# A hybrid decoder layer on one core: where the plain loads, the accumulating DMAs and the last merged quarter's epilogue stand

## The chip, the cores and the metric

The kernel runs on one core of a Trainium2 chip. The metric is the device time of one execution, in microseconds; the time before is 816.44 us, the median of three runs (816.44 to 817.08). The core has five engines with their own in-order streams of instructions: TensorE (PE in the profile), VectorE (DVE), ScalarE (ACT), GpSimd (POOL) and SyncE (SP). SP, ACT and POOL also issue DMAs here, and a DMA stands in its issuer's stream like any other instruction.

## What is computed

One layer on a sequence of 256 tokens of width 2048, all in float32:

```python
h = rmsnorm(x, norm_mix_g)
u = h @ w_in                                  # 12,288 columns
c_g, b_g, xa, za, q, fl, iv, og, ga, gb = split(u)   # ga, gb: 2048 each
ya = b_g * causal_dwconv3(c_g * xa, conv_w) * silu(za)
o  = hgrn2_chunked(silu(q), (1 - lb) * sigmoid(-fl), iv, log_f)
yb = rmsnorm_heads(o) * hg_norm_g * silu(og)
m  = sigmoid(ga) * (ya @ w_a_out) + sigmoid(gb) * (yb @ w_b_out)
x  = x + m @ w_o
x  = x + sigmoid(rmsnorm(x, ple_norm_g) @ w_ple_gate) * (p @ w_ple_proj)
out = rmsnorm(x, final_norm_g)
```

The time goes into the matrix products: 256 rows against some 150 MB of weights.

## The kernel before

**Products.** Each float32 operand is held as a high part and a low part, and a product of two is three matmuls: high by high, high by low, low by high (`triple`, L1038 to L1040). A matmul has 128 tokens as its stationary side and 512 weight columns as its moving side. A chunk is 256 rows of the contraction by 512 columns, for both halves of the tokens: 2 x 2 products, 12 matmuls. The program walks a list of chunks, `items`, in the order of the parts of `w_in`, then `w_a` and `w_b`, then `w_o` (kind "O", four quarters of columns of eight chunks each), then the last gate.

**Weights.** `load` sends 1 MB for two chunks (512 KB in the first stage) from SP's queue into one of three buffers `raw`. `split` calls `cut`: ScalarE writes the high part (`whi`, L169), VectorE the low part (`wlo`, L170). This runs three chunks (`LEAD`) ahead of the products, further ahead at the end. TensorE has only products to do and goes from one chunk to the next without a pause, as long as the parts are there.

**Units of seven products.** For three of the four quarters of `ga` and `gb` (j = 1, 2, 3), five of the eight chunks (c = 0, 2, 3, 5, 6) are "units", kind "S": the 2 x 2 blocks of tokens and contraction, and the `ga` and `gb` columns beside each other, are computed by seven products for eight, after Strassen and Winograd. For it sums of weights are needed, and sums of token blocks. The three other chunks (c = 1, 4, 7) are plain (kind "C"). There are 15 units.

- Sums of weights, `combine_weights`, called two items ahead of the unit. `A` (`sA`, two buffers) and `B` (`sB`, two buffers) are loaded on SP's queue. `X` (`sT`, three buffers) is formed by `add_by_dma` on POOL's queue: a plain load of 512 KB (L157) and then a DMA of 512 KB that adds to it on arrival (L163), which waits for the load to have landed. VectorE makes two sums (L701), and then `X`, `B` and `A` are each cut into parts: `thi`, `tlo` of `X`, `bhi`, `blo` of `B`, `thi`, `tlo` of `A`. There is one pair of `bhi`, `blo`. At its end `combine_weights` calls `add_by_dma()` for the next unit that has none; the first are called for at `begun + 3`, `+ 5` and `+ 7`, where `begun` is the last chunk before the units.
- Sums of tokens, `token_sums`: once, before the units, four sums for each of the five chunks, in high and low parts, `shi` and `slo`, from the parts `xh`, `xl` of the tokens (`hT`).
- `unit_products` issues the seven products of a unit in the order of `names_of`: two with `whi`, `wlo`, then the one that multiplies `bhi`, `blo` (the block B22 of the weights) with the fourth token sum, then four more.

**The merge.** When the products of `w_b` for quarter j are complete, `ep_bb` (L778) multiplies them by the gate (`gb`, L782), adds the other branch (L786), and has the result `m`. It must be turned so that its columns lie on partitions before it can multiply `w_o`. The turn goes through DRAM: four writes (`to_dram`, L304), one read back (L315), and a transposition in squares on VectorE (L308). Quarters 0 to 2 are parked in DRAM and come back later (`unpark`). The last, j = 3, goes through `turned` at once; then `put_m` makes `mh` (ScalarE, L775) and `ml` (VectorE, L776), which are the stationary sides of the products with `w_o`. The chunks of "O" use the quarters in order, so that the last quarter comes with contraction blocks 12 to 15.

**Order.** Each epilogue is a generator; `advance` lets every live one go a step, once for each chunk. What stands between two `yield`s stands together in the streams of the engines. Each engine runs its stream in order. The planner of the language then orders the instructions of each engine by its own estimate, except where dependencies are put in by hand: between `begun` and eight chunks after the last quarter of the branch products began (`parked`), `pinned` fixes the order of ScalarE and VectorE to the order in which the program was written. SP's stream in the order of the built program is, near the last quarter: a load of `w_o`, the four writes of the turn, a load of `w_o`, the readback, three loads of `w_o`.

Of the kernel before, what the change touches and what calls it, by code (L numbers as in the profile page):

```python
# [9 lines left out]
F32 = mybir.dt.float32  # L10
F32R = mybir.dt.float32r
AF = mybir.ActivationFunctionType
ALU = mybir.AluOpType
PSUM = bass.MemoryType.PSUM

P = 128
# [7 lines left out]
CW = 512  # L24
# [7 lines left out]
SEVEN = [()] + 3 * [(0, 2, 3, 5, 6)]  # L32
# [15 lines left out]
def hybrid_kernel(ctx, tc, xT, x, pT, prm, gfin, masks, w_in, w_a, w_b, w_o, w_pg, w_pp, out):  # L48
    nc = tc.nc
# [9 lines left out]
    pools, closers = {}, {}  # L59
# [13 lines left out]
    state = {"tmp": "tmp1"}  # L73
# [3 lines left out]
    def nm(s):  # L77
        uid[0] += 1
        return f"{s}_{uid[0]}"

    def t4(tag="t4", bufs=None):
        bufs = bufs or {"tmp1": 8, "tmp2": 1, "tmp3": 5}[state["tmp"]]
        return pools[state["tmp"]].tile([P, 1024], F32, tag=tag, bufs=bufs, name=nm(tag))
# [12 lines left out]
    pair_sums = {}  # L96
# [9 lines left out]
    items = []  # L106
# [16 lines left out]
    def raw_of(pos):  # L123
        it = items[pos]
        if it["raw"] not in loaded:
            if it["kind"] == "S":
                t = tuple(
                    pools["st"].tile([P, n, CW], F32, tag=tag, bufs=2, name=nm(tag)) for tag, n in (("sA", 2), ("sB", 1))
                )
            else:  # L130
                t = wp.tile([P, 2, 2 * CW], F32, tag="raw", bufs=3, name=nm("raw"))
            loaded[it["raw"]] = t
        return loaded[it["raw"]]
# [18 lines left out]
    def add_by_dma(behind=None):  # L152
        pos = next((n for n, it in enumerate(items) if it["kind"] == "S" and n not in pair_sums), None)
        if pos is not None:
            w, g, c = items[pos]["w"]
            X = pair_sums[pos] = pools["st"].tile([P, 2, CW], F32, tag="sT", bufs=3, name=nm("sT"))
            d = nc.gpsimd.dma_start(out=X.rearrange("p n x -> p (n x)"), in_=w[g + 1, :, c, :])  # L157
            if behind is not None:
                tc.add_manual_dep(
                    d.ins, behind.name,  # L160
                    mybir.DependencyInfo(mybir.DependencyClass.Sync, mybir.DependencyReason.DATA), reason="order",
                )
            nc.gpsimd.dma_start(out=X, in_=w[g : g + 2, :, c, :CW].rearrange("n p x -> p n x"), accum_op=ALU.add)  # L163

    def pair_of(pool, n, tags=("whi", "wlo"), width=2 * CW):
        return tuple(pool.tile([P, width], F32R, tag=tag, bufs=n, name=nm(tag)) for tag in tags)
# [18 lines left out]
    def combine_weights(pos):  # L185
        st = pools["st"]
        (A, B), X = raw_of(pos), pair_sums[pos]
        add(A[:, 0], X[:, 0], B[:, 0])
        add(A[:, 1], A[:, 0], A[:, 1])
        ts = []  # L190
        for n, src in enumerate((X, B, A)):
            hi, lo = pair_of(st, 1, ("bhi", "blo"), CW) if n == 1 else pair_of(st, 3, ("thi", "tlo"))
# [9 lines left out]
    begun = next(n for n, it in enumerate(items) if it["kind"] == "ga" and it["last"])  # L202
# [7 lines left out]
    prm_t = const.tile([P, PRM_N], F32, name="prm_t")  # L210
    praw = pools["tmp1"].tile([P, 1024], F32, tag="X", bufs=4, name="praw")[:, : 2 * T]
    pop = pools["tmp1"].tile([P, 1024], F32R, tag="X", bufs=4, name="pop")
# [76 lines left out]
    def blocks(ap):  # L289

        return ap.rearrange("p (c b e) -> p c b e", b=4, e=32)
# [5 lines left out]

        return ap.rearrange("p (b c t e) -> p t c b e", b=4, c=4, t=NT)[:, t]

    def to_dram(src, tag, bufs):  # L300
        d = dram.tile([P, 4, T], F32, tag=tag, bufs=bufs, name=nm(tag))
        to = d.rearrange("(b i) a x -> a i b x", b=4)
        for a in range(4):
            nc.sync.dma_start(out=to[a], in_=src[32 * a : 32 * a + 32, :].rearrange("i (b x) -> i b x", b=4))  # L304
        return d

    def square_turn(dst, src):
# [1 line left out]
            out=dst.rearrange("p (k a e) -> p a k e", a=4, e=32), in_=src.rearrange("p (a k e) -> p a k e", a=4, e=32)  # L309
        )  # L310

    def turned(src, lag, dst=None):
        d = to_dram(src, "turn", 3)
        yield
        nc.sync.dma_start(out=src, in_=d.rearrange("p a x -> p (a x)"))  # L315
        for _ in range(lag):
            yield
        dst = t4() if dst is None else dst
        square_turn(dst, src)
        return dst  # L320
# [413 lines left out]

    def token_sums():
        nu = len(SEVEN[1])
        state["S"] = pair_of(pools["st"], 1, ("shi", "slo"), nu * 4 * P)
        state["S"] = tuple(v.rearrange("p (u s t) -> p u s t", u=nu, s=4) for v in state["S"])
        yield
        yield  # L740
        for first, n in TOGETHER:
            yield
            F, S = (
                pools["st"].tile([P, 2 * CW], F32R, tag=tag, bufs=3, name=nm(tag))[:, : n * 4 * P].bitcast(F32)
                for tag in ("thi", "tlo")
            )
            c = SEVEN[1][first]
            hi, lo = (v[:, 2 * c : 2 * (c + n), :] for v in state["hT"])
            Fv = F.rearrange("p (k t) -> p k t", t=T)
            nc.vector.tensor_tensor(out=Fv, in0=hi.bitcast(F32), in1=lo.bitcast(F32), op=ALU.add)  # L750
            yield
            Fv = F.rearrange("p (u r b t) -> p u r b t", u=n, r=2, b=2)
            Sv = S.rearrange("p (u s t) -> p u s t", u=n, s=4)
            a11, a12, a21, a22 = Fv[:, :, 0, 0], Fv[:, :, 1, 0], Fv[:, :, 0, 1], Fv[:, :, 1, 1]
            s1, s2, s3, s4 = (Sv[:, :, i] for i in range(4))
            for out, u, v, op in (
                (s1, a21, a22, ALU.subtract), (s2, s1, a11, ALU.subtract),
                (s3, a11, a21, ALU.subtract), (s4, a12, s2, ALU.add),
            ):
                nc.vector.tensor_tensor(out=out, in0=u, in1=v, op=op)  # L760
            hi, lo = (v[:, first : first + n] for v in state["S"])
            nc.scalar.activation(out=hi, in_=Sv, func=AF.Copy)
            nc.vector.tensor_tensor(out=lo, in0=Sv, in1=hi.bitcast(F32), op=ALU.subtract)
            yield

    def ep_a(j, psum):
# [11 lines left out]
    def ep_bb(j, psum):  # L778
        ga, gb = state["ga"], state["gb"]
        for t in range(NT):  # L780
            s = slice(t * CW, (t + 1) * CW)
            nc.vector.tensor_tensor(out=gb[:, s], in0=gb[:, s], in1=psum[t], op=ALU.mult)  # L782
        m = t4()
        for t in range(NT):
            s = slice(t * CW, (t + 1) * CW)
            nc.vector.tensor_tensor(out=spread(m, t), in0=blocks(ga[:, s]), in1=blocks(gb[:, s]), op=ALU.add)  # L786
        if j == 3:
            m = yield from turned(m, 3, back())
            put_m(j, m)
        else:  # L790
            state["m", j] = to_dram(m, f"m{j}", 1)
            yield

    def back():
        return pools["back"].tile([P, 1024], F32, tag="back", bufs=5, name=nm("back"))
# [259 lines left out]
    def names_of(it):  # L1055
        if it["kind"] == "C":
            return [("c", it["n"], t) for i in range(2) for t in range(NT)]
        return ["P1", ("c", 0, 0), ("c", 1, 0), "P5", "P7", "P6", ("c", 0, 1)]

    def into(name, op, part):  # L1060
        left[name] -= 1
# [3 lines left out]
    def unit_products(pos):  # L1065
        it = items[pos]
        c, h = it["c"], state["hT"]

        def x_of(r, t):
            return tuple(v[:, 2 * c + r, t * P : (t + 1) * P] for v in h)  # L1070

        hi, lo = parts.pop(pos)
        halves = [(hi[:, i * CW : (i + 1) * CW], lo[:, i * CW : (i + 1) * CW]) for i in range(2)]
        names = names_of(it)
        if it["kind"] == "C":
            for n, name in enumerate(names):
                into(name, x_of(n // 2, n % 2), halves[n // 2])
            return
        b22, t1, t3, t2, t4_ = sums.pop(pos)
        s1, s2, s3, s4 = (tuple(v[:, SEVEN[1].index(c), i] for v in state["S"]) for i in range(4))  # L1080
        for name, op, part in zip(names, (x_of(0, 0), x_of(1, 0), s4, s1, s3, s2, x_of(1, 1)),
                                  (halves[0], halves[1], b22, t1, t3, t2, t4_)):
            into(name, op, part)

    def pinned(start):
# [16 lines left out]
    for pos, it in enumerate(items[:last_group]):  # L1102
        mark = len(nc.cur_bb.bb.instructions)
        kind, j, c, last = (it[n] for n in ("kind", "j", "c", "last"))
        _, _, w, g, opname = groups[it["gi"]]
# [60 lines left out]
        else:  # L1166
            if c == 0:
                psum = [bank("s" if kind == "PP" and j >= 2 else "g") for _ in range(NT)]
            hi, lo = parts.pop(pos)
            for i in range(2):  # L1170
                k = 2 * c + i
                s = slice(i * CW, (i + 1) * CW)
# [10 lines left out]
        if pos == begun:  # L1183
            finish()
            second_part()
            active.append(token_sums())
        if pos in (begun + 3, begun + 5, begun + 7):
            add_by_dma(state["splits"][0])
        if kind == "O" and j == 0 and c == nch - 3:
            finish()  # L1190
# [23 lines left out]
    for t, halves in ((0, (0, 1)), (1, (0,)), (1, (1,))):  # L1214
        bk, n = bank("g"), CW // 2
        for c in range(nlast):
# [3 lines left out]
            hi, lo = parts[last_group + c]  # L1220
            for i in range(2):
                k = 2 * c + i
                s = slice(i * CW + halves[0] * n, i * CW + (halves[-1] + 1) * n)
# [83 lines left out]
```

## Time and profile before

| | |
|---|---|
| time, median of three runs | 816.44 us (816.44 to 817.08) |
| time of the profiled execution | 816.5 us |
| its span in the trace | 814.7 us |
| TensorE busy | 803.2 us, 4059 matmuls |
| VectorE, ScalarE busy | 589.2 us, 459.4 us |
| read from HBM, written to it | 184.19 MB, 13.63 MB |
| DMA of 512 KB on POOL's queue, median from issue to landing | 8.5 us (30 issues) |
| a 1 MB load of `w_o` on SP's queue, the same | 6.1 us (16 issues) |
| a write of 128 KB for a turn, the same | 2.8 us (60 issues) |

The span begins with the first instruction of the trace and ends with the last. A row of a timeline gives the start, the duration, the engine (SPq, ACTq are the parts that issue DMAs), the line of the kernel, the operation, and what it writes and reads. In brackets stands the time that the engine sat idle just before, and what released it. The chain of waits goes back from the last instruction, at each step to what released it. A window row gives the stretch, the busy time of the engines with the number of instructions, the granted clock of TensorE, the mean share of the DMA engines that were busy, and GB/s.

### The profile page before, as it was taken

How to read it: one execution, taken by the hardware profiler on the slowest of the kernel's cores; microseconds unless marked ns; L12 is line 12 of the kernel's file. 1: busy time of each engine (PE TensorE's matmuls, PEld its weight loads, DVE VectorE, ACT ScalarE, POOL GpSimd, SP SyncE). 2: the span in 40 equal slices, each digit the busy share in tenths (PEclk: the TensorE clock that was granted, in tenths of full speed). 3: DMA queues.
4: the chain of work that ended last, by engine and by line, in shares of the span. 5: the costliest groups of instructions: out<-in, count | busy, mean ns of one | idle time of the engine just before them, and what ended most of it. 6: DMA issues, size and time to landing. Idle time of an engine off the chain costs nothing.

```text
span 814.7 us, 10651 instructions
## 1 busy us (share of the span) xinstructions
PE 803.2 (99%) x4059; PEld 665.4 (82%) x4059; DVE 589.2 (72%) x745; ACT 459.4 (56%) x614; POOL 48.5 (6%) x57
## 2 busy tenths in 40 slices
PE   9999999999999999999999999999999999999995
PEld 6888888888888888888888878888888788888885
DVE  7746588767766498767679968987988756677932
ACT  7576476466565466456455546556554546566623
POOL 1000000001000000010011110110100000001210
PEclk9999999999999999999999999999999999999998
DMA  9988555648867555648789989998944888777802
GB/s 339 392 307 288 197 201 175 233 139 267 252 237 249 198 175 196 207 157 269 259 296 282 286 268 297 284 280 260 283 163 177 291 300 300 255 274 298 276 34 103
DMA packets 52659, 198.52 MB, mean 244 GB/s; under 512 B 6784, under 2 KB 16256, under 8 KB 37888
## 3 DMA queue, kind: packets, MB, share of 16 engines
q1 hardware_dynamic: 45504, 180.54, 63.6%
q0 software_dynamic: 6240, 15.73, 8.2%
q10 hardware_dynamic: 864, 1.57, 0.5%
q8 instruction: 31, 0.51, 0.2%
q14 instruction: 20, 0.16, 0.1%
HBM read 184.19 MB, written 13.63 MB: 243 GB/s over the span
## 4 chain that ended last, share of the span: by engine, by line
PE 85%; DVE 7%; issue 4%; DMA 2%; ACT 2%; POOL 0%; POOLq 0%; DVEq 0%; ACTq 0%
PE g L1038 26%; PE g L1039 26%; PE g L1040 25%; DVE wlo L170 3%; PE s L1039 2%; PE s L1040 2%; PE s L1038 2%; DMA sT<-in_w_in 1%; DMA raw<-in_w_o 1%; PE s L484 1%; DVE sA L701 1%; ACT whi L169 0%; DVE tlo L170 0%; PE s L932 0%; DVE back L308 0%
## 5 line engine op out<-in xcount | busy, mean ns | idle before, releaser
L170 DVE TENSOR_TENSOR wlo<-raw,whi 128x1024 fp32r<-128x1024 f32 (+1 forms) x264 | 319.9, 1229 | 159.9 <-ACT whi L169 158.0
L169 ACT ACTIVATE whi<-raw 128x1024 fp32r<-128x1024 f32 (+1 forms) x264 | 272.9, 1051 | 208.1 <-PE g L1040 175.2
L1038 PE MATMUL g<-whi,xh 128*128 128x512 f32 (+1 forms) x738 | 283.8, 385 | 0.0
L1039 PE MATMUL g<-wlo,xh 128*128 128x512 f32 (+1 forms) x738 | 283.7, 384 | 0.0
L1040 PE MATMUL g<-whi,xl 128*128 128x512 f32 (+1 forms) x738 | 283.6, 384 | 0.0
L1040 PEld LDWEIGHTS g<-whi,xl 128*128 128x128 f32 x738 | 138.7, 188 | 27.8
L1038 PEld LDWEIGHTS g<-whi,xh 128*128 128x128 f32 x738 | 138.7, 188 | 27.5
L1039 PEld LDWEIGHTS g<-wlo,xh 128*128 128x128 f32 x738 | 138.7, 188 | 27.1
L1039 PE MATMUL g<-wlo,mh 128*128 128x512 f32 x128 | 49.9, 390 | 0.3 <-DVE wlo L170 0.3
L1038 PE MATMUL g<-whi,mh 128*128 128x512 f32 x128 | 49.6, 389 | 0.0
L1040 PE MATMUL g<-whi,ml 128*128 128x512 f32 x128 | 49.5, 389 | 0.0
L1040 PE MATMUL s<-whi,xl 128*128 128x512 f32 x84 | 32.7, 389 | 0.0
L1038 PE MATMUL s<-whi,xh 128*128 128x512 f32 x84 | 32.7, 389 | 0.0
L1039 PE MATMUL s<-wlo,xh 128*128 128x512 f32 x84 | 32.7, 389 | 0.0
L169 ACT ACTIVATE thi<-sA 128x1024 fp32r<-128x1024 f32 x15 | 15.9, 1063 | 25.0 <-DVE sA L701 21.3
L1039 PEld LDWEIGHTS g<-wlo,mh 128*128 128x128 f32 x128 | 24.0, 188 | 5.6 <-DVE wlo L170 0.7
L1038 PEld LDWEIGHTS g<-whi,mh 128*128 128x128 f32 x128 | 24.0, 188 | 5.1
L1040 PEld LDWEIGHTS g<-whi,ml 128*128 128x128 f32 x128 | 24.0, 188 | 5.0
L1039 PE MATMUL g<-wlo,ybTh 128*128 128x512 f32 x64 | 24.9, 389 | 0.0
L1040 PE MATMUL g<-whi,ybTl 128*128 128x512 f32 x64 | 24.9, 389 | 0.0
L1038 PE MATMUL g<-whi,yaTh 128*128 128x512 f32 x64 | 24.9, 389 | 0.0
L1039 PE MATMUL g<-wlo,yaTh 128*128 128x512 f32 x64 | 24.9, 389 | 0.0
(215 smaller groups left out, 910.2 us busy)
## 6 DMA issues: line engine op xcount, KB each, us to landing
raw<-in_w_in SPq DMA_DIRECT2D x66, 1024.0 KB, 5.0
raw<-in_w_o SPq DMA_DIRECT2D x16, 1024.0 KB, 6.1
raw<-in_w_pg SPq DMA_DIRECT2D x16, 1024.0 KB, 5.7
sT<-in_w_in POOLq DMA_DIRECT2D x30, 512.0 KB, 8.5
raw<-in_w_in SPq DMA_DIRECT2D x28, 512.0 KB, 6.9
raw<-in_w_a SPq DMA_DIRECT2D x8, 1024.0 KB, 6.4
raw<-in_w_b SPq DMA_DIRECT2D x8, 1024.0 KB, 7.7
turn<-t SPq DMA_DIRECT2D x60, 128.0 KB, 2.8
```

Of the source, the lines that this page charges most:

```text
L169: a = nc.scalar.activation(out=hi, in_=src, func=AF.Copy)
L170: v = nc.vector.tensor_tensor(out=lo, in0=src, in1=hi.bitcast(F32), op=ALU.subtract)
L484: nc.tensor.matmul(out, X[:, 0, h, s], X[:, 1, h, t], start=True, stop=True, tile_position=(0, i * n))
L701: nc.vector.tensor_tensor(out=out, in0=a, in1=b, op=ALU.add)
L1038: nc.tensor.matmul(psum, oh, hi, start=first, stop=False)
L1039: nc.tensor.matmul(psum, oh, lo, start=False, stop=False)
L1040: nc.tensor.matmul(psum, ol, hi, start=False, stop=last)
```

## The change

1. `add_by_dma` issues the plain load of a unit, and behind it the accumulation of the unit before it, which it kept in `state["adding"]`. With no more unit to load it issues the accumulation alone. There are four buffers `sT` and three `sB`, and one more call at `begun + 9`. POOL's stream becomes load 0, load 1, accumulation 0, load 2, accumulation 1, and so on. From the fifth on a load waits until `X` of the unit four before it has been cut.
2. For the room, `token_sums` keeps three of the four sums in `shi`, `slo`; the fourth goes into the places of `xh`, `xl` (the second half of the tokens, the first block of each unit's contraction) which the units' products don't read otherwise. For each of the three groups of chunks ScalarE and VectorE get one more instruction.
3. The seven products of a unit start with the one of B22 and the fourth sum; the two with `whi`, `wlo` follow.
4. In `ep_bb`, for j = 3, a `yield` stands behind the multiplication and one behind the addition, and the lag ahead of the square turn is two for three. The four writes are issued by ScalarE, the readback by POOL.

In the built program SP's stream near the last quarter is then: `w_o` loads without a break, four loads of `x` and the load of the final gain, and the next `w_o` load; the four writes stand on ScalarE ahead of the `whi` of the following pair of chunks. On VectorE one `wlo` stands between the multiplications and the additions, and the square turn stands directly ahead of `ml`. On TensorE, five matmuls of the second chunk of the next group of columns come ahead of the first that uses the last quarter, beyond those that did before.

```diff
-                    pools["st"].tile([P, n, CW], F32, tag=tag, bufs=2, name=nm(tag)) for tag, n in (("sA", 2), ("sB", 1))
+                    pools["st"].tile([P, n, CW], F32, tag=tag, bufs=bufs, name=nm(tag))
+                    for tag, n, bufs in (("sA", 2, 2), ("sB", 1, 3))
...
-            X = pair_sums[pos] = pools["st"].tile([P, 2, CW], F32, tag="sT", bufs=3, name=nm("sT"))
+            X = pair_sums[pos] = pools["st"].tile([P, 2, CW], F32, tag="sT", bufs=4, name=nm("sT"))
             d = nc.gpsimd.dma_start(out=X.rearrange("p n x -> p (n x)"), in_=w[g + 1, :, c, :])
...
-            nc.gpsimd.dma_start(out=X, in_=w[g : g + 2, :, c, :CW].rearrange("n p x -> p n x"), accum_op=ALU.add)
+        if "adding" in state:
+            w, g, c = items[state["adding"]]["w"]
+            X = pair_sums[state.pop("adding")]
+            with tc.issue_after(d.ins) if pos is not None else ExitStack():
+                nc.gpsimd.dma_start(
+                    out=X, in_=w[g : g + 2, :, c, :CW].rearrange("n p x -> p n x"), accum_op=ALU.add
+                )
+        if pos is not None:
+            state["adding"] = pos
...
-    def to_dram(src, tag, bufs):
+    def to_dram(src, tag, bufs, queue=nc.sync):
...
-            nc.sync.dma_start(out=to[a], in_=src[32 * a : 32 * a + 32, :].rearrange("i (b x) -> i b x", b=4))
+            queue.dma_start(out=to[a], in_=src[32 * a : 32 * a + 32, :].rearrange("i (b x) -> i b x", b=4))
...
-    def turned(src, lag, dst=None):
-        d = to_dram(src, "turn", 3)
+    def turned(src, lag, dst=None, queues=(nc.sync, nc.sync)):
+        d = to_dram(src, "turn", 3, queues[0])
         yield
-        nc.sync.dma_start(out=src, in_=d.rearrange("p a x -> p (a x)"))
+        queues[1].dma_start(out=src, in_=d.rearrange("p a x -> p (a x)"))
...
-        state["S"] = pair_of(pools["st"], 1, ("shi", "slo"), nu * 4 * P)
-        state["S"] = tuple(v.rearrange("p (u s t) -> p u s t", u=nu, s=4) for v in state["S"])
+        state["S"] = pair_of(pools["st"], 1, ("shi", "slo"), nu * 3 * P)
+        state["S"] = tuple(v.rearrange("p (u s t) -> p u s t", u=nu, s=3) for v in state["S"])
...
-            hi, lo = (v[:, first : first + n] for v in state["S"])
-            nc.scalar.activation(out=hi, in_=Sv, func=AF.Copy)
-            nc.vector.tensor_tensor(out=lo, in0=Sv, in1=hi.bitcast(F32), op=ALU.subtract)
+            sums_of = tuple(v[:, first : first + n] for v in state["S"])
+            fourth = tuple(v[:, 2 * c : 2 * (c + n) : 2, P:] for v in state["hT"])
+            for (hi, lo), src in ((sums_of, Sv[:, :, :3]), (fourth, Sv[:, :, 3])):
+                nc.scalar.activation(out=hi, in_=src, func=AF.Copy)
+                nc.vector.tensor_tensor(out=lo, in0=src, in1=hi.bitcast(F32), op=ALU.subtract)
...
             nc.vector.tensor_tensor(out=gb[:, s], in0=gb[:, s], in1=psum[t], op=ALU.mult)
+        if j == 3:
+            yield
...
         if j == 3:
-            m = yield from turned(m, 3, back())
+            yield
+            m = yield from turned(m, 2, back(), (nc.scalar, nc.gpsimd))
...
-        return ["P1", ("c", 0, 0), ("c", 1, 0), "P5", "P7", "P6", ("c", 0, 1)]
+        return [("c", 1, 0), "P1", ("c", 0, 0), "P5", "P7", "P6", ("c", 0, 1)]
...
-        if pos in (begun + 3, begun + 5, begun + 7):
+        if pos in (begun + 3, begun + 5, begun + 7, begun + 9):
             add_by_dma(state["splits"][0])
```

More of the change, by code (lines that the diff above doesn't have):

```diff
@@ L1079, in unit_products @@
         b22, t1, t3, t2, t4_ = sums.pop(pos)
-        s1, s2, s3, s4 = (tuple(v[:, SEVEN[1].index(c), i] for v in state["S"]) for i in range(4))
-        for name, op, part in zip(names, (x_of(0, 0), x_of(1, 0), s4, s1, s3, s2, x_of(1, 1)),
-                                  (halves[0], halves[1], b22, t1, t3, t2, t4_)):
+        s1, s2, s3 = (tuple(v[:, SEVEN[1].index(c), i] for v in state["S"]) for i in range(3))
+        s4 = x_of(0, 1)
+        for name, op, part in zip(names, (s4, x_of(0, 0), x_of(1, 0), s1, s3, s2, x_of(1, 1)),
+                                  (b22, halves[0], halves[1], t1, t3, t2, t4_)):
             into(name, op, part)
```

## The prediction, made before the changed kernel ran

> **What bounds the kernel now.** I read the page first, then TensorE's waits, then its busy time by stretches, then the timelines and the chain of waits around each gap.
>
> ```profile
> PE 803.2 (99%) x4059; PEld 665.4 (82%) x4059; DVE 589.2 (72%) x745; ACT 459.4 (56%) x614; POOL 48.5 (6%) x57
> ```
> ```profile
> 460.00:480.00 20.00, 18.95 (x84) 1.00 0.77 209
> 480.00:640.00 160.00, 160.00 (x707) 1.00 0.80 254
> 640.00:660.00 20.00, 19.71 (x87) 1.00 0.93 331
> 660.00:800.00 140.00, 140.00 (x642) 1.00 0.67 237
> 800.00:814.70 14.70, 5.99 (x50) 0.78 0.34 126
> ```
> ```profile
> PE s L932 <- DVE warm L928: 1.5, 1, 1.5
> PE s L1039 <- DVE blo L170: 1.0, 1, 1.0
> PE g L1039 <- DVE wlo L170: 0.3, 1, 0.3
> ```
>
> TensorE is busy for 803.2 of 814.7 us. Of the 11.5 us idle, 1.5 lie at the head, 8.7 in the tail (14.70 - 5.99), and 1.05 and 0.29 in two stretches; the granted clock is 1.00 in those. No matmul is removed, so only the last two are to be had. What each costs is more than its idle time, since a matmul that waits inside a product also starts its successor late:
>
> ```profile
> 474.79 0.39 PE L1038 MATMUL s<-bhi,shi 128*128 128x512 f32 x1
> 476.23 0.50 PE L1039 MATMUL s<-blo,shi 128*128 128x512 f32 x1 [1.04 <-DVE blo L170]
> 476.56 0.40 PE L1040 MATMUL s<-bhi,slo 128*128 128x512 f32 x1
> ```
> ```profile
> 646.84 0.61 PE L1038 MATMUL g<-whi,mh 128*128 128x512 f32 x2
> 647.74 0.50 PE L1039 MATMUL g<-wlo,mh 128*128 128x512 f32 x1 [0.29 <-DVE wlo L170]
> 648.08 0.40 PE L1040 MATMUL g<-whi,ml 128*128 128x512 f32 x1
> ...
> 650.15 0.40 PE L1038 MATMUL g<-whi,mh 128*128 128x512 f32 x1
> ```
>
> Columns of the timeline: start, duration, what ran, and in brackets the idle time before it. Starts of matmuls normally lie 0.226 us apart (160 us for 707, the row of 480 to 640). Stall 1: from 474.79 to 476.56 is 1.77 for two starts (0.45), so **1.32 us**. Stall 2: from 646.84 to 648.08 is 1.24 for three starts (0.68), so **0.56 us**. Together 1.88 us, 0.23% of the time. This is the most the change can gain.
>
> Where they come from, by the chain of waits, then POOL's, VectorE's and SP's timelines:
>
> ```profile
> 452.36 0.59 POOL sT L157
> ...
> 461.51 11.32 DMA sT<-in_w_in
> ```
> ```profile
> 473.02 0.69 DVE L701 TENSOR_TENSOR sA<-sT,sB 128x512 f32<-128x512 f32 x1 [4.48 <-DMA sT<-in_w_in]
> ```
> ```profile
> 639.21 6.05 DMA raw<-in_w_o
> ...
> 645.37 1.07 ACT whi L169
> ...
> 646.46 1.24 DVE wlo L170
> ```
> ```profile
> 637.33 1.78 SPq L304 DMA_DIRECT2D turn<-t  x4
> 639.21 0.39 SPq L150 DMA_DIRECT2D raw<-in_w_o  x1
> ...
> 642.84 0.34 SPq L315 DMA_DIRECT2D t<-turn  x1
> ```
>
> Stall 1: POOL issued a unit's plain load at 452.36, waited 8.6 us for it, and only then issued the accumulation, which took 11.32 us; VectorE sat 4.48 us for it. Stall 2: the 1 MB load of `w_o` stood on SP's queue behind the four writes of the last quarter, and landed 6.05 us after 639.21.
>
> **The change part by part.**
>
> *The accumulation.* A unit's accumulation now follows the plain load of the next unit, and its own load was issued one unit before. The accumulation that went at 461.51 can go right behind the issue at 452.36, at some 453.5. With its 11.32 us it lands at 464.8, and 4.48 us of idle VectorE ended at 473.02, so VectorE could first use it at 468.5: margin 3.7. What POOL is moved past is one plain load at a time; each waits for `tlo` of the unit four back, as the one before waited for that of three back. If the load beside it slows the accumulation by as much as a whole load (9.2 us, 452.36 to 461.51), it lands at 474.0, 1.2 later than before. I take the margin, which is nearest to the 11.32 seen with loads beside it: gain **1.32**, bounds a loss of 1.2 and the whole gain.
>
> *The B22 product first.* It needs `bhi`, `blo` six matmuls (1.36 us) earlier. The tile view of `blo`:
>
> ```profile
> L170 DVE TENSOR_TENSOR blo<-sB,bhi x15: 684/685/693, 441.8 to 596.7; 128x512 fp32r<-128x512 f32 x15
> L1039 PE MATMUL s<-blo,shi x15: 389/389/499, 445.1 to 600.1; 128*128 128x512 f32 x15
> ```
>
> The first pair is ready at 442.5 and used at 445.1, the last at 597.4 and used at 600.1: 2.6 and 2.7 us, so some 1.2 stays. The three more ScalarE and VectorE instructions for the fourth sum (at most 0.69 each, as `blo`) lie in the same cover. Cost 0; if a unit lacked it, at most 1.36 for that unit.
>
> *SP's queue.* With the writes gone the `w_o` load goes out when its buffer is free, behind the previous `wlo`, 1.9 us earlier (637.3 for 639.21). Then whi and wlo are 1.9 earlier against 0.9 us of stall seen: gain **0.56**, with about 1 us to spare; bounds 0 and 0.56. Four loads of `x` and the final gain now stand ahead of a later `w_o` load; with the DMA share at 0.67 from 660 on I take 0, at worst a stall of stall 2's size, 0.56.
>
> *The last quarter's epilogue.* Here is the price.
>
> ```profile
> 634.82 1.28 DVE L782 TENSOR_TENSOR gb<-gb,g 128x512 f32<-128x512 f32 x2
> 636.02 1.29 DVE L786 TENSOR_TENSOR t<-ga,gb 128x512 f32<-128x512 f32 x2
> ...
> 647.60 1.24 DVE L308 STREAM_TRANSPOSE back<-t 128x1024 f32<-128x1024 f32 x1
> ```
> ```profile
> 648.88 1.07 ACT L775 ACTIVATE mh<-back 128x1024 fp32r<-128x1024 f32 x1 [0.78 <-DVE back L308]
> 648.88 0.82 ACTq L993 DMA_DIRECT2D xs<-in_x  x2
> ```
>
> `mh` was complete at 649.95, and in program order the matmul at 650.15 is the first to use it: it was 0.2 us from being a stall itself. Now, on the same clock:
> - A `wlo` (1.24, as at 646.46, with its start overlapped 1.2) stands between the products and the sum, so the sum ends at 638.5 for 637.3.
> - Four writes on ScalarE's queue cost four issues of 0.41 (0.82 for two): issued by 640.2. The next `whi` on ScalarE waits up to 1.2 us behind them; it has three chunks of lead, 8.2 us.
> - The last write landed, before, when the readback could go, 642.84 - 639.11 = 3.7 after its issue. Nearest rows for the bounds:
>
> ```profile
> raw<-in_w_o SPq DMA_DIRECT2D x9, 1024.0 KB, 6.1
> ...
> turn<-t SPq DMA_DIRECT2D x4, 128.0 KB, 2.6
> t<-turn SPq DMA_DIRECT2D x1, 512.0 KB, 4.1
> ```
>
>   2.6 (the median write) below, 6.1 above (as long as the 1 MB load that now runs beside them). I take 3.7: 643.9.
> - The readback goes from POOL. POOL's timeline has the same 512 KB as plain loads:
>
> ```profile
> 514.11 0.59 POOL L157 DMA_DIRECT2D sT<-in_w_in  x1 [3.71 <-DVE tlo L170]
> 520.62 1.18 POOL L163 DMA_DIRECT2D sT<-in_w_in  x1 [5.91 <-DMA sT<-in_w_in]
> ...
> 565.87 0.59 POOL L157 DMA_DIRECT2D sT<-in_w_in  x1 [10.15 <-DVE tlo L170]
> 570.86 1.18 POOL L163 DMA_DIRECT2D sT<-in_w_in  x1 [4.40 <-DMA sT<-in_w_in]
> ```
>
>   6.5 and 5.0 us; I take 5.7. Below 4.1 (SP's readback), above 9.2 (the load at 452.36). Landed at 649.6.
> - Turn and `mh` take 2.35 (647.60 to 649.95): `mh` at 651.95; low 640.2 + 2.6 + 4.1 + 2.35 = 649.25, high 640.2 + 6.1 + 9.2 + 2.35 = 657.85.
>
> TensorE wants it at 650.15, less stall 2 (0.56), plus five matmuls of the next group that the new order puts ahead (1.13): 650.7. New stall: **1.2 us**, between 0 and 7.1. Behind the turn on VectorE stands only `ml` and then a `wlo` for a later chunk; behind `mh` on ScalarE two loads and a `whi`, both covered by that same lead unless the stall passes some 4 us.
>
> The Trainium skill, page "DMA: Bandwidth & Descriptors", section "Queues, rings and completion order", says that each DMA engine takes turns, a packet at a time, between the queues that have work for it. By it the writes on ScalarE's queue share the engines with the 1 MB load, where on SP's they went ahead of it; the sum by it is the slower rival's, and no row here shows two such queues at once. The same page's section on the software path gives about 2.0 us plus the bytes over 436 GB/s, an estimate of 3.2 us for the readback, by which there would be no stall and the sum would be 814.6; the 5.0 to 6.5 us above speak against it.
>
> Sum, against the profiled execution's own 816.5 us (span 814.7 and 1.8 around it; the median of the runs is 816.44, the same within 0.1): 816.5 - 1.32 - 0.56 + 1.2 = **815.8 us**.
>
> **The rivals.**
> - *Both stalls go and the quarter is in time.* It needs the chain 1.2 us shorter than my sum: writes as the median (2.6) or a readback like SP's (4.1). For it: the load that shares the engines with them now starts 1.9 us sooner, and is that much further on. Against it: before, with the better queue, 0.2 us was left. 816.5 - 1.88 = 814.6.
> - *Slower: the quarter becomes the bound.* The writes share the engines with the 1 MB load and take its 6.1, and the readback, among the loads that follow, 6.5: 640.2 + 6.1 + 6.5 + 2.35 = 655.15, a stall of 4.4: 816.5 - 1.88 + 4.4 = 819.0. It decides once the stall passes 1.88. For it, the DMA engines there are full already; the window view has
>
> ```profile
> 640.00:642.00 2.00, 2.00 (x10) 1.65 (x10) 1.85 (x2) 0.40 (x1) 0.00 (x0) 1.00 1.03 228
> ```
>
>   a DMA share of 1.03 at 228 GB/s. Against it, the transfers have been seen at 3.7 and 4.1 in this very place.
> - *The change doesn't do what it says in the first stage.* The accumulation, beside a load, lands late again, or B22 first makes a new stall of up to 1.36: stall 1 is replaced. 816.5 - 0.56 + 1.2 = 817.1. Against it the margin of 3.7 us.
>
> **How the numbers follow.** A measurement of this kernel tells about 0.2% (1.63 us) from no change. My forecast, a stall between 0.25 and 3.5, has 0.38: no change. The quarter in time has 0.33: faster. The slower rival has 0.19, and of the last (0.10) I count 0.05 as slower and 0.05 as no change. So faster 0.33, same 0.43, slower 0.24. The likeliest case's own range is 814.9 to 818.1. For 8 in 10 the range goes from just under the full gain, 814.4, to 818.8, nearly all of the slower rival's sum; the high end of the chain (7.1 us, 821.7) is left out.
>
> **What would show it.** Stall 1 right: TensorE's waits have no `blo`, and no accumulation waits for its own load for 8 us. Stall 2 right: the `w_o` load starts next to 637.3 and no wait for `wlo` follows. The quarter right: a wait of TensorE for `mh` of about 1.2 us near 651, the readback on POOL taking 5 to 6.5 us. Wrong: no wait there (faster), or one over 3.5 us (slower), or a wait for `blo` or `tlo` anywhere among the units.

## The result, and the profile after

The changed kernel takes 822.81 us, the median of six runs (821.85 to 826.62); before, beside it, 816.22 (815.64 to 817.08). The ratio is 1.0088, 95% interval 1.0066 to 1.0110: slower by 0.9%, some 6.6 us, outside the range forecast.

First the page's engine line of the changed kernel, then TensorE's waits, then its busy time by stretches (us, busy time and matmuls, granted clock, share of the DMA engines, GB/s):

```profile
PE 804.2 (98%) x4059; PEld 665.9 (81%) x4059; DVE 590.3 (72%) x748; ACT 458.7 (56%) x617; POOL 48.9 (6%) x58
```
```profile
PE g L1052 <- ACT mh L786: 7.2, 1, 7.2
PE s L946 <- DVE warm L942: 1.5, 1, 1.5
```
```profile
440.00:480.00 40.00, 40.00 (x179) 1.00 1.00 303
480.00:640.00 160.00, 160.00 (x707) 1.00 0.73 238
640.00:660.00 20.00, 12.79 (x50) 0.83 0.91 332
```

Both old waits, for `blo` and for `wlo`, are gone: 440 to 480 is full. One new wait is there, for the last quarter's `mh`, and it is 7.2 us long. The granted clock falls to 0.83 in that stretch. The timeline of TensorE shows both costs:

```profile
649.11 0.39 PE L1053 MATMUL g<-wlo,mh 128*128 128x512 f32 x1
656.71 0.79 PE L1052 MATMUL g<-whi,mh 128*128 128x512 f32 x1 [7.21 <-ACT mh L786]
657.30 0.63 PE L1053 MATMUL g<-wlo,mh 128*128 128x512 f32 x1
657.73 0.63 PE L1052 MATMUL g<-whi,mh 128*128 128x512 f32 x1
...
660.03 0.40 PE L1052 MATMUL g<-whi,mh 128*128 128x512 f32 x1
```

From 649.11 to 656.71 is 7.60 where 0.23 is due: 7.37 us lost. Then matmuls start 0.43 us apart for 0.23, and eight starts take 3.32 us for 1.81: another 1.51. The two stalls that went saved 1.88. 7.37 + 1.51 - 1.88 = 7.0, and the spans differ by 821.7 - 814.7 = 7.0: the whole loss is in this one place.

The chain of waits says what was late:

```profile
637.09 0.34 ACTq L313
...
638.43 8.73 DMA turn<-t
...
647.83 6.47 DMA t<-turn
654.32 1.26 DVE back L317
655.60 1.06 ACT mh L786
656.71 0.79 PE g L1052
```
```profile
637.09 2.68 ACTq L313 DMA_DIRECT2D turn<-t  x4
```
```profile
635.88 12.48 SPq L151 DMA_DIRECT2D raw<-in_w_o  x4
```

One of the four writes landed 8.73 us after its issue, at 647.16; counted from the end of the four issues (637.09 + 2.68 = 639.77) that is 7.4 us, where before it was 3.7. The readback on POOL took 6.47. SP meanwhile sends one 1 MB load after the other. A view of the DMA queues over 642.5 to 644 shows how the two share (queue, packets, MB, share of the 16 engines; q1 is SP's queue, q10 ScalarE's):

```profile
DMA packets 123, 0.57 MB, mean 378 GB/s; under 512 B 3, under 2 KB 61, under 8 KB 61
...
q1 hardware_dynamic: 64, 0.51, 88.1%
q10 hardware_dynamic: 59, 0.06, 11.2%
```

64 packets of SP's queue and 59 of ScalarE's: in this stretch the queues move as many packets each, as if they took turns, one for one. But a packet of the load is 8 KB and one of the writes 1 KB, so the writes get 11% of the engines' time here. It isn't so all the way. From 640 to 641 few packets of loads were moving, 20 against 298 of the writes, and the writes had 81.3% of the engines. By 642.5, 445 of their 576 packets were through; what is late is the rest, beside the loads issued at 639.4 and 643.4.

The Trainium skill, page "DMA: Bandwidth & Descriptors", section "Queues, rings and completion order", has the rule of turns between queues, packet by packet; the counts of the stretch agree. The section puts some 9 to 17 descriptors into a packet; the turns seen here are of single transfers of 8 KB and 1 KB, as the second experiment shows.

### The profile page after: what moved, and what is told of

Its sections match the earlier page's. It is cut to its first block, busy times and chain, and to the rows that moved or that the text cites. A ratio compares the mean times of both kernels' runs of the same rounds, so it can differ in the third digit from the quotient of the medians.

```text
span 821.7 us, 10659 instructions
## 1 busy us (share of the span) xinstructions
PE 804.2 (98%) x4059; PEld 665.9 (81%) x4059; DVE 590.3 (72%) x748; ACT 458.7 (56%) x617; POOL 48.9 (6%) x58
## 4 chain that ended last, share of the span: by engine, by line
PE 90%; DVE 3%; issue 2%; DMA 2%; ACT 1%; ACTq 0%; POOLq 0%; POOL 0%
PE g L1052 27%; PE g L1054 27%; PE g L1053 27%; PE s L1053 3%; PE s L1054 3%; PE s L1052 3%; DVE wlo L179 2%; DMA turn<-t 1%; DMA t<-turn 1%; DVE back L317 1%; PE s L493 1%; ACT mh L786 1%; PE s L946 0%; PE s L594 0%; ACT whi L178 0%
## 5 line engine op out<-in xcount | busy, mean ns | idle before, releaser
L1052 PEld LDWEIGHTS g<-whi,mh 128*128 128x128 f32 x128 | 24.4, 191 | 12.6 <-ACT mh L786 7.6
```

The costliest lines, as they stand in the source:

```text
L1052: nc.tensor.matmul(psum, oh, hi, start=first, stop=False)
```

## The experiments

The variants start from the changed kernel, except where the kernel before is named; times are medians, ratios go against runs of the kernel before on the same chip. Theory A: the writes are late because their queue takes turns with the loads of SP's queue. Its rivals: the readback on POOL and the extra steps (B), the later sum (C), ScalarE's queue itself (D).

**Writes back on SP's queue, the readback on POOL's.**

```diff
-            m = yield from turned(m, 2, back(), (nc.scalar, nc.gpsimd))
+            m = yield from turned(m, 2, back(), (nc.sync, nc.gpsimd))
```

> The changed kernel with the last quarter's four writes back on SP's queue (behind the w_o load that was issued first, ahead of the next one); the readback stays on POOL, the extra steps stay. Theory A (the writes are late because ScalarE's queue shares the DMA engines with two 1 MB loads on SP's queue): the last write lands about 4 us after its issue for 8.7, the readback takes 6 to 6.5 us as before, TensorE waits about 2.5 us for mh (7.2 - 4.7), time 817 to 818 us. Theory B (the readback on POOL and the extra steps are the price): the writes gain little or the chain stays long, the wait for mh is 5 us or more, time 820 or more.

817.63 us, ratio 1.0019 (1.0008 to 1.0029). Its waits, then its chain:

```profile
PE g L1053 <- DVE wlo L179: 1.8, 1, 1.8
```
```profile
639.16 3.87 DMA turn<-t
...
643.70 7.15 DMA t<-turn
...
650.87 0.04 DVE back L317
...
652.04 1.19 DVE wlo L179
```

The last write lands 3.87 us after its issue for 8.73, as A has it. The wait is not for `mh` but for a `wlo` that stands behind the square turn on VectorE: with other queues the planner also put matmuls in another order. In the built programs the first matmul with the last quarter's `mh` stands 13 places (2.9 us) later than in the changed kernel.

**The readback alone on SP's queue** (`(nc.scalar, nc.sync)`; the order of TensorE, VectorE and ScalarE up to `mh` as in the changed kernel).

> The changed kernel with the readback alone back on SP's queue; the writes stay on ScalarE's. Theory A: the writes still land some 8.7 us after the last issue; the readback at best 4.1 us and no POOL issue, so TensorE waits 4 to 7 us, time 819 to 823. Theory B: the wait for mh is under 2 us, time below 817.

820.15 us, ratio 1.0038 (1.0018 to 1.0057).

```profile
PE g L1052 <- ACT mh L786: 4.2, 1, 4.2
```
```profile
639.72 8.13 DMA turn<-t
...
647.93 3.75 DMA t<-turn
```

The writes are as late as before (8.13), the readback takes 3.75 for 6.47 and starts without POOL's 0.67 (647.16 to 647.83 in the changed kernel). So POOL's share of the wait is some 3 us and the rest the larger one; B falls as the sole cause. The ten runs go from 815.98 to 821.69, and the one profiled (821.61) is among the slowest; the three fastest, 815.98 to 817.20, leave little room for such a wait, so the write need not be this late each time.

This trace also shows the turns themselves. With the readback on SP's queue no third load follows, and from 645.8 to 647.4 the engines are nearly empty, in the view of the DMA queues (GB/s in 40 slices of 0.04 us):

```profile
GB/s 0 0 26 205 0 0 51 410 0 0 0 26 205 0 26 26 230 0 0 26 205 0 0 26 0 0 0 0 26 205 0 0 0 0 0 0 0 26 0 0
q1 hardware_dynamic: 10, 0.06, 8.6%
q10 hardware_dynamic: 14, 0.01, 2.1%
```

In a slice, 26 GB/s is one packet of 1 KB and 205 one of 8 KB. They mostly come in pairs, a small one and then a large one, less than two of the 16 engines' worth (10.7%), and the last write lands at 647.85. So the write waits for a few packets that still take turns with 8 KB ones while most engines have nothing to do; the mean share of 11% doesn't measure that. Why these are behind the others, no run here shows.

**Both on SP's queue, the extra steps kept** (`(nc.sync, nc.sync)`).

> The changed kernel with writes and readback on SP's queue, the extra steps kept. Theory A: writes about 4 us, readback 4 to 6 us, wait for mh 0 to 2 us, time 814.5 to 816.5. Theory C (the later sum, by one wlo, and the five matmuls put ahead are themselves the price): a wait of 5 us or more stays, time above 820.

814.90 us, ratio 0.9989 (0.9979 to 0.9998): faster than both kernels. No wait but the first one of the program is left to TensorE. C falls as it was put, with a wait of 5 us or more. The SP rows:

```profile
637.36 2.69 SPq L313 DMA_DIRECT2D turn<-t  x4
640.16 0.39 SPq L151 DMA_DIRECT2D raw<-in_w_o  x1
644.07 0.34 SPq L324 DMA_DIRECT2D t<-turn  x1
```

4.0 us from the end of the issues to the readback, even with one 1 MB load sent ahead of the writes. It isn't all due to that: `mh` starts only at 652.39 and ends at 653.43, which would be late by some 4 us in the changed kernel's order. Here the planner put the matmul that needs it 19 places, 4.3 us, later. From the first write's issue to the end of `mh` it is 16.1 us here, 19.6 in the changed kernel and 12.6 in the kernel before. The writes and the readback take 5.4 us less than in the changed kernel (3.4 and 2.0), but the turn, which stands behind a `wlo` on VectorE here, gives 1.9 back. So 3.5 of the 7.4 us are gone; the rest is a chain that is longer than before on SP's queue too, and only this order of TensorE hides it. To that extent C stands.

**The whole epilogue of before**, parts 1 to 3 of the change alone:

```diff
-        if j == 3:
-            yield
...
-            yield
-            m = yield from turned(m, 2, back(), (nc.scalar, nc.gpsimd))
+            m = yield from turned(m, 3, back())
```

> The changed kernel with the whole epilogue of before (no extra steps, lag 3, everything on SP): parts 1 to 3 of the change alone. All theories: stall 1 (1.32 us) is gone, stall 2 (0.56 us) stays, no wait for mh over 0.5 us: 816.2 - 1.3 = 814.9 us, 0.16% below before. If the accumulation or the B22 product first had a hidden price, it shows here as a time at or above 816.2.

815.75 us, ratio 0.9992 (0.9983 to 1.0002). The profile is as expected, a wait for `wlo` and none for `blo`; the time gained 0.2 us for 1.3 in the median, and the interval holds both.

**Longer packets, everything else in place.** The order of all instructions is that of the changed kernel.

```diff
-            queue.dma_start(out=to[a], in_=src[32 * a : 32 * a + 32, :].rearrange("i (b x) -> i b x", b=4))
+            s = slice(32 * a, 32 * a + 32)
+            queue.dma_start(out=d[s].rearrange("p a x -> p (a x)"), in_=src[s, :])
```

(for ScalarE's queue alone)

> The changed kernel, with the four writes of the last quarter laid out in DRAM row by row, so that each of the 128 rows goes as one run of 4 KB for four of 1 KB; bytes, queue and order of all instructions stay (the turn then reads a wrong layout, so the last quarter of m is not the layer's). Theory A (two queues take turns packet for packet, and a 1 KB packet waits for an 8 KB one each time): the last write lands 4 to 5.5 us after its issue for 8.7, the wait for mh is 3.5 to 5 us, time 818 to 820. Theory D (it is the bytes that share, or ScalarE's queue that is slow): the write lands after 8 us or more, time 822 to 823.

821.65 us, ratio 1.0077 (1.0054 to 1.0101). The tile's landing times (the slowest of the four writes and the readback), then TensorE's waits:

```profile
DMA to landing us min/median/max: 4.9/5.1/6.3
```
```profile
PE g L1056 <- ACT mh L790: 3.6, 1, 3.6
PE s L950 <- DVE warm L946: 1.5, 1, 1.5
PE s L1057 <- DVE blo L179: 0.6, 1, 0.6
```

With a quarter of the packets and the same bytes the slowest write takes 6.3 us for 8.7, and the wait for `mh` is half. 2.4 us of that are the write's; another 1.2 come from the readback, 5.3 for 6.47. That is A's direction, short of its 5.5, and D's "8 us or more" is out. The time is not what A forecast: the slow clock after the wait was left out of the expectation, and this profiled execution has a `blo` wait besides.

**One load held** until the writes have landed (the second of those beside them; the third stands behind it in SP's queue):

```diff
-                nc.sync.dma_start(out=raw, in_=w[g, :, c : c + 2, :])
+                d = nc.sync.dma_start(out=raw, in_=w[g, :, c : c + 2, :])
+                for before in state.pop("hold", ()):
+                    tc.add_manual_dep(
...
```

> The changed kernel, with one wait more: the second 1 MB load of w_o that ran beside the writes is held until the four writes have landed; writes on ScalarE's queue, readback on POOL's. Theory A: without that load the last write lands 3 to 4.5 us after its issue, the readback, beside the held load, takes 6 to 7.5, and TensorE waits 2.5 to 4.5 us for mh or for a weight behind it: 817 to 819. Theory D (ScalarE's queue is slow by itself): the write lands after 7 us or more, and the time is 822 or more.

821.90 us, ratio 1.0076 (1.0056 to 1.0095).

```profile
639.02 5.01 DMA turn<-t
...
644.69 8.15 DMA t<-turn
```

The write takes 5.01 for 8.73, but the held load and those behind it now run beside the readback, which takes 8.15 for 6.47. What was given up at one place is paid at the next: the wait is 5.2 us. A's forecast had the direction, but its sizes (4.5 for the write, 7.5 for the readback, 819 for the time, at most) are all passed. From 642.3 to 643.6 the last 34 packets run alone, at 7.0% of the 16 engines, about one engine's worth: here too a few packets are behind the others.

**Both loads held**, a probe of the writes alone: the first load goes behind the writes in the program, too.

> The changed kernel, with both 1 MB loads of w_o that ran beside the four writes held until the writes have landed; a probe, its time is no matter (the weights come late). Theory A: alone on the DMA engines the last write lands 2 to 3 us after the end of the issues (7.4 in the changed kernel). If ScalarE's queue is slow by itself: 4 us or more.

```profile
638.18 2.80 ACTq L319 DMA_DIRECT2D turn<-t  x4
642.96 1.96 SPq L152 DMA_DIRECT2D raw<-in_w_o  x3
```

The loads, which waited for the writes, go at 642.96, 2.0 us after the end of the issues (640.98). ScalarE's queue isn't slow: 2.0 us with no load, 4.5 with one (639.48 to 644.03), 7.3 with two (640.52 to 647.85, the readback alone on SP's queue), 7.4 in the changed kernel, where three ran beside the writes in turn (issued at 635.9, 639.4 and 643.4). D falls, A stands. The readback, among the released loads, took 8.25, and the one run 825.27 us.

**Once more the changed kernel**, no edit.

> The changed kernel, profiled once more: by theory A the late write is no accident. The last write lands 6 us or more after its issue, the wait for mh is 5 to 9 us, and after it matmuls start 0.43 us apart for some 3 us. If the 7.2 us were an accident of one execution: a wait under 4 us.

824.34 us in one run; the same place again, with matmuls 0.43 us apart behind the wait, and a wait of 0.2 us for `blo` besides:

```profile
PE g L1052 <- ACT mh L786: 7.4, 1, 7.4
```
```profile
638.98 8.71 DMA turn<-t
...
648.36 6.69 DMA t<-turn
```

**The old order of the accumulations** on the version with both on SP's queue: `add_by_dma` of before, three buffers `sT`.

> As e3_both_sp, with add_by_dma as before the change (plain load and its own accumulation in a row, three buffers sT); the B22 product stays first, the three buffers sB stay. If the order of POOL's DMAs is what took stall 1 away, the wait for blo comes back, and with B22 first by up to 1.36 us longer than before: 1.3 to 2.7 us over e3_both_sp, 816.2 to 817.6 us. If something else in the change took it away (three buffers sB, say): 814.9.

814.69 us, ratio 0.9985 (0.9971 to 1.0000), no wait for `blo`: against my expectation, the order of POOL's DMAs was not needed. So each part among the units was tried alone on the same version, and the kernel before profiled twice more.

> The kernel before, profiled once more. If stall 1 belongs to the kernel: the wait for blo of about 1.0 us comes again at the same unit, and the accumulation ahead of it lands 11 us or more after its issue. If it is an accident of one execution's transfers (e7_old_adds had the old order and no such wait): no wait for blo, VectorE waits less than 2 us for sT, and stall 2 alone is left.

> The kernel before, profiled a third time, for the same question: wait for blo again (it belongs to the kernel) or not (an accident).

817.37 and 816.89 us, one run each; `blo` is waited for both times, with the same cause. VectorE's wait, of the first and of the second:

```profile
DVE sA L701 <- DMA sT<-in_w_in: 3.7, 1, 3.7
...
```
```profile
DVE sA L701 <- DMA sT<-in_w_in: 4.1, 1, 4.1
...
```

So stall 1 is in all three profiles of the kernel before; stall 2 is in two of them, since the execution of 817.37 us has no wait for `wlo`. They need not be in every execution: the fastest runs of the kernel before take 814.64 us, as little as a version without any such wait, and its medians beside the variants are 815.5 to 816.5. That fits the 1.0 us that the version without a wait gains in the median (814.90 for 815.94), where 1.88 were forecast.

**The product order of before** (B22 third) on the version with both on SP's queue:

> As e3_both_sp, with the seven products of a unit in the order of before (B22 third). If B22 first is without price and without gain, as predicted: 814.9 us, equal to e3_both_sp within 0.1%, no wait for blo in either. If it costs something at the units: 814.3 or less; if it is needed: a wait at the next unit's splits, 815.5 or more.

814.72 us, ratio 0.9985 (0.9976 to 0.9995), for 814.90 with B22 first: no price that the times can show, and no gain.

**One part each**, from the same version: the third `sB` alone (old accumulations, B22 third), B22 first alone (old accumulations, two `sB`), the new accumulations alone (two `sB`, B22 third).

> As e7_old_adds (plain load and its accumulation in a row, writes and readback of the last quarter on SP), with the B22 product third as before the change: of the parts among the units only the third buffer sB is left. If the third buffer took stall 1 away in e7_old_adds: 814.7 us, no wait for blo. If the B22 product first did: a wait for blo of about 1 us, 815.9 to 816.2.

> As e7_old_adds, with two buffers sB: of the parts among the units only the B22 product first (and the fourth sum's place) is left. If B22 first took stall 1 away: 814.7 us, no wait for blo. If the third buffer did: a wait for blo of 1.3 to 2.7 us, 816.0 to 817.4.

> As e3_both_sp, with two buffers sB and B22 third: of the parts among the units only the load ahead of the accumulation and the fourth buffer sT are left. As I read the trace of before this alone is enough: no wait for blo, VectorE waits for no accumulation, 814.7 to 814.9 us. If not: 816 or more.

815.14 (ratio 0.9996, 0.9986 to 1.0005), 815.42 (0.9994, 0.9977 to 1.0011) and 814.84 us (0.9991, 0.9982 to 1.0001). None has a wait of TensorE for `blo`. VectorE's wait for the accumulation, with the third `sB` and with B22 first:

```profile
DVE sA L702 <- DMA sT<-in_w_in: 2.3, 1, 2.3
```
```profile
DVE sA L702 <- DMA sT<-in_w_in: 1.9, 1, 1.9
```

With the new accumulations alone there is no such wait at all. So only they take the cause away; in the two others the accumulation is still late, by about 2 us for 4, and TensorE's cover was just enough in the one execution profiled. Those two executions were the second fastest of ten each (814.36 and 814.68, where the slowest are 816.34 and 818.65), so it isn't shown that the wait stays away in the others. The intervals of the three overlap, so the times don't rank them.

**The two extra steps alone**, put into the kernel before, writes and readback on SP:

```diff
+        if j == 3:
+            yield
         m = t4()
...
-            m = yield from turned(m, 3, back())
+            yield
+            m = yield from turned(m, 2, back())
```

> The kernel before with the two extra steps in the last quarter's epilogue and the lag of two alone; writes and readback on SP, everything among the units as before the change. If the steps take stall 2 away and stall 1 is mostly an accident: 814.7 to 815.0 us, as e3_both_sp and e7_old_adds, no wait for mh or wlo in the O stage. If stall 1 belongs to the kernel before: 815.9 to 816.3, with a wait for blo.

815.04 us, ratio 0.9983 (0.9975 to 0.9992), with waits of 0.5 us for `blo` and 0.2 for a `whi` left and none for `mh`. This small edit has the gain of the O stage without the loss. Again the order of TensorE is a part of it: `mh` ends at 654.5 here, 4.6 us later than in the kernel before, and nothing waits for it, so its first use has moved back by over 4 us, too. This version, the one with both on SP's queue, and that one with B22 third are the three that beat both kernels with the whole of their intervals.

## Why the prediction was wrong

- *Stall 1, gain 1.32*: gone in the changed kernel, as forecast. The reason given, the order of the accumulations, is sufficient by the version that has it alone. Whether it is the only one stays open: in the one profile of each, `blo` wasn't waited for either with the third `sB` alone or B22 first alone, though there VectorE still waited.
- *B22 first and the fourth sum at no cost*: right by the medians for B22 first, 814.90 with and 814.72 without; the fourth sum's new place stood in both. But the reading under it, a cover of 2.6 us, took the first and the last of fifteen units. At the fifth, that of stall 1, `blo` ends in the changed kernel at 473.2 and is used at 473.6, and three of the eleven profiles with B22 first have a short wait for it (0.2, 0.6 and 0.6 us). None of the three variants of the changed kernel with B22 third has one.
- *Stall 2, gain 0.56*: gone, as forecast, with the load at 637.2 for 637.3 on the old clock (635.88 + 1.32).
- *The last quarter*: that TensorE would wait for `mh` was right, and the step that failed is the sum of the chain. TensorE ran out of other work where it was expected: at 649.34 in this profile (649.11 + 0.23), which with stall 1's 1.32 added is 650.66, for 650.7. On the same clock `mh` ended at 657.98 (655.60 + 1.06 + 1.32) for 651.95, past the high bound of 657.85. The terms: the end of the writes' issues came 0.9 later (641.1 for 640.2), since the fourth issue took 1.33 for 0.41; "I take 3.7" for the last write's landing was 7.4 (643.9 became 648.5), **the mis-sized term**, above even its bound of 6.1; POOL's start cost 0.67 that had no term; the readback was 6.47 for 5.7. (The 6.5 and 5.0 under that 5.7 run to POOL's next issue; the loads themselves had landed after 6.2 and 4.7.)
- Why 3.7 was the wrong row: it was measured on SP's queue, where the writes stood ahead of the load. The prediction saw that the load would now run beside them and took its 6.1 us as the bound. But three loads ran beside them in turn, and the last of their 1 KB packets took turns with 8 KB ones; the length of one load was no bound.
- *No term for the clock*: 1.51 us of 7.0 came from half-speed matmuls after the wait. With it and the right landing (a wait of 1.2 + 3.7 = 4.9) the sum would have been 816.5 - 1.88 + 4.9 + 1.5 = 821.0; the three smaller terms, 0.9, 0.67 and 0.8, make up the rest of the 823.5 measured in that execution.
- *The rivals*: the slower one named the mechanism and the place, and priced it at 819.0 with 0.19. It put the landing at 6.1 and had no clock term either.
- *The rule cited for the slower rival* agreed with the counts, at the size of single transfers; the one that would have made POOL's readback take 3.2 us did not: 5.3 to 8.3 us in six profiles, against 3.75 and 5.1 on SP's queue.

## What to carry to other kernels

A short strided DMA that is on the critical path should not be put on a second queue beside a stream of large loads: the queues take turns by packets, so its 1 KB packets pay for 8 KB ones. Put it in the loads' own queue, ahead of or between them, and look at how many packets it has, not only at its bytes. Then look where the planner has put the first instruction that needs it: with both on SP's queue, and with the two steps alone, `mh` came later than before, and only the later first use hid it. Where a wait of TensorE may come back, count the half-speed matmuls behind it too.

## What was not expected of the hardware

After a pause TensorE's matmuls started 0.43 us apart for 0.23, and not after long pauses only. Pauses of 7.2 and 4.2 us cost another 1.5 and 2.3 us. A pause of 1.8 us, in the version with the writes on SP, was followed at first by full speed and then by half:

```profile
653.28 0.50 PE L1053 MATMUL g<-wlo,mh 128*128 128x512 f32 x1 [1.77 <-DVE wlo L179]
653.61 0.39 PE L1054 MATMUL g<-whi,ml 128*128 128x512 f32 x1
...
655.66 0.63 PE L1054 MATMUL g<-whi,ml 128*128 128x512 f32 x1
656.09 0.63 PE L1052 MATMUL g<-whi,mh 128*128 128x512 f32 x1
...
657.95 0.39 PE L1052 MATMUL g<-whi,mh 128*128 128x512 f32 x1
```

The thirteen steps from 653.28 to 657.95 take 4.67 us for 2.95: 1.7 us, as much as the pause itself. The granted clock is 1.00 from 653.2 to 654.2 and 0.53 from 654.6 to 657.8. The pauses of about 1 us for `blo` in the kernel before show 0.3 at most. The Trainium skill, page "TensorE: Matmul & The Clock Gate", section "Part 1: The HAM clock gate", warns of idle gaps over some 3.4 us; the 0.43 us agrees with its half rate, but in this one profile the half rate followed a pause of 1.8 us. That the pause alone brought it on isn't shown.
